# A written instruction order from w_out's last norm to gate_up's first pair, with GpSimd making two of the four sums of h2

## The chip, the cores and the metric

The kernel runs on one core of one Trainium2 chip. The core has a matrix engine (TensorE, PE in the profile; PEld is its load of the stationary operand), three engines for elementwise work (VectorE = DVE, ScalarE = ACT, GpSimd = POOL), a queue engine that here only issues DMAs (SyncE = SP), and DMA engines that move data between DRAM and SBUF. Each engine works off its own list of instructions in order; instructions of different engines wait for each other through semaphores. The metric is the device time of one execution in microseconds (us); lower is better.

## The reference, cut to what matters

One residual block: a mixer and a feed-forward network, each between two RMS norms.

```python
def rmsnorm(x, g):
    return x * lax.rsqrt(jnp.mean(x * x, axis=-1, keepdims=True) + RMS_EPS) * g

m = mixer(rmsnorm(x, norm_mix_pre), ...)          # ends with merged @ w_out
x = x + rmsnorm(m, norm_mix_post)
h = rmsnorm(x, norm_ffn_pre)
g, u = jnp.split(h @ w_gate_up, 2, axis=-1)        # [1024, 1024] @ [1024, 2 * 2816]
x = x + rmsnorm((jax.nn.silu(g) * u) @ w_down, norm_ffn_post)
```

All in float32, sequence 1024, model width 1024, hidden width 2816. The change lies between the product with w_out and the first columns of gate_up.

## The kernel before, in words

**Products.** TensorE multiplies in a reduced float32, so each operand is split into a high part (a copy by ScalarE, `copy`) and a low part (source minus high, by VectorE, `sub`); `split` (118) does both, and `mm3` (123) adds high x high, high x low and low x high into one PSUM bank. An operand's low is needed from the third matmul of a product on. `prod` (445) is four such triples: 12 matmuls 128x512, one *product* in what follows.

**gate_up as pairs.** The columns of w_gate_up are taken in 22 pairs f: 128 gate columns and the 128 up columns that belong to them. One pair is a 2x2 block product with the two halves of the sequence, done with seven products in place of eight (Strassen's scheme in Winograd's form). Its weight operands are A11 and A12 (gate columns, lower and upper half of the contraction), A22 and four sums S1 to S4; its operands of h are B11, B21, B22 and four sums T1 to T4. `prep_first` (397) loads the gate columns (`raw`, 512 KB) and splits them; `prep_rest` (408) loads the up columns, makes S1 to S4 (into `sx`, `raw` and `s4`) and splits them. `strassen` (474) does the products in the order S2, S1, S3, S4, A22 and joins them by additions into c12, c22 and c21; with each bank that is read, a bank comes free for a later product. B11 and B21, the first half of the sequence, stand as `hah`/`hal`; B22 as `hch`/`hcl`; T1 to T4 as `hth`/`htl` with blocks 0 to 3.

**The stage of the change.** w_out is done in eight tiles of 128 rows: `e_mm` (1179) makes a tile's two banks `pm`, `e_norm` (1198) follows one tile later: two Squares by ScalarE out of PSUM, the factor (`rms_scale` 177, a Sqrt by ScalarE among five small ones by VectorE), two multiplications with the gain (`tt`), the addition to x, a store of x2 by GpSimd's queue, a third Square, a second factor, one multiplication, and on TensorE eight transposes into two banks, which ScalarE copies to `um` (h, transposed). Tile 7 is the last.

After tile 5 all of B11 and B21 are there, so the products A11 and A12 of the first seven pairs (NPRE = 7) can be done before the second half of the sequence is. `f_first(f)` (1232) does that for pair f: load, split, A11's product, a copy of the bank to `c21`, A12's product added into the same bank, a copy to `c12`, both stored to `pre_dram` by GpSimd's queue. Four of them are written ahead of tile 7's norm, three behind it, between the quarters of `h2_sums` (1267): for each quarter (128 columns of each half of the sequence) VectorE makes two sums u (T1, T2, in `sx`, each needs the one before) and two sums w (T3, T4, in `c22`), all four are split into `hth`/`htl`, and B22's quarter into `hch`/`hcl`.

Then comes the loop over the 22 pairs (1311). For f < NPRE GpSimd's queue loads the two kept products back (1313 to 1316, tiles `c21` and `c11`), `Pairs` prepares the rest of two pairs ahead, and `strassen` does the five products left. The results go through a Sigmoid on ScalarE into `sgf` (1326) and two multiplications on VectorE.

**What sets the order.** A scheduler orders each engine's list by its own estimate of readiness, except where instructions are marked by `tc.keep_in_program_order`: then they stay as written. All engine calls go through the helper `InOrder` (65 to 78), which marks while `strict[0]` is set; so every recorded instruction bears its line, L73. `strict` is on up to the end of the attention part and is set off at 1139, ahead of w_out; from there on, and so in the whole stage, the scheduler decides. Buffers bind as well: `raw` has 3, `hi` 4, `lo` 3, `sx` 1, `s4` 1, and `c21`, `c12`, `c22` 2 each; PSUM has six banks here. SyncE's list holds the loads of weights and x, GpSimd's the stores and the loads of `pre_dram`; an issue waits in its list for the buffer that it fills, or for the landing of what it reads back, and holds up what stands behind it.

Of the kernel before, what the change touches and what calls it, by code (L numbers as in the profile page):

```python
# [17 lines left out]
P = 128  # L18
# [27 lines left out]
def block_kernel(  # L46
# [13 lines left out]
    w_down: bass.AP,  # L60
    out: bass.AP,
):
    strict = [False]

    class InOrder:


        def __init__(self, engine):
            self.engine = engine

        def __getattr__(self, name):
            def call(*args, **kw):
                ins = getattr(self.engine, name)(*args, **kw)  # L73
# [7 lines left out]
    nc = SimpleNamespace(  # L81
        **{e: InOrder(getattr(bass_nc, e)) for e in ("tensor", "vector", "scalar", "gpsimd", "sync")}
    )
    x2d = x[0]
    o2d = out[0]
# [20 lines left out]
    def add(o, a, b):  # L106
        nc.vector.tensor_tensor(o, a, b, op=ALU.add)
# [7 lines left out]
    def copy(o, a):  # L115
        nc.scalar.activation(o, a, AF.Copy)
# [280 lines left out]
    def prep_first(src1, there=None):  # L397

        if there is None:
            r1 = raw_t()  # L400
            nc.sync.dma_start(r1, kmaj(src1))
            h1, l1 = hi_t(), lo_t()
            split(h1, l1, r1)
        else:
            r1, h1, l1 = there
        return dict(A11=(h1[:, LO], l1[:, LO]), A12=(h1[:, UP], l1[:, UP])), r1

    def prep_rest(src2, r1):

# [48 lines left out]
    def t_(tmp, name):  # L458
        return tmp.tile([P, NC], F32, tag=name, name=name)
# [335 lines left out]
    for ij, (kind, j, _, _) in enumerate(jobs):  # L795
        if ij == 2:
            logf_pre = forget_sums()
        if ij == 4:
            forget_store(*logf_pre)
        if ij < 2:  # L800
            if ij == 0:
                heads = [
                    prep_first(wcols(a), t) for (_, _, a, _), t in zip(jobs, ((r0, h0, l0), None))
                ]
                firsts = [
                    strassen_first(w, h1b, psm, pp, n == 0) for n, (w, _) in enumerate(heads)
                ]
            (w, r1), (c11, p1) = heads[ij], firsts[ij]
            w = {**w, **prep_rest(wcols(jobs[ij][3]), r1)}
            if ij == 1:  # L810
                pairs.q.append(pairs.prep(*pairs.srcs.popleft()))
            _, c12, c21, c22 = strassen(w, h1b, psm, pp, p1)
        elif ij < len(jobs) - 1:
            if ij == 12:
                k_load(0)
                q_load(0)
                cb_of(0, 0)
                cb_of(0, 1)
            c11, c12, c21, c22 = strassen(pairs.get(), h1b, psm, pp)
        else:  # L820
            w = pairs.get()
            psm_close()
            strict[0] = True
            pss, pss_close = pool("pss", space=PSUM)
            c11, c12, c21, c22 = last_pair(w)
        if kind == "qk":
            so = pp.tile([P, NC], F32, tag="so", name="so")
            copy(so, c11)
            for r, c, t in ((0, n1, so), (0, n2, c12), (1, n1, c21), (1, n2, c22)):
                nc.gpsimd.dma_start(qk_dram[j][r, :, c], t)  # L830
        elif kind == "z":
            zt = z_tile("zt")
            mul(zt[:, n1], c21, c11)
            mul(zt[:, n2], c12, c22)
            zts[j] = zt
        elif kind == "gb":
            for m, parts in ((j, (c11, c12)), (j + 1, (c21, c22))):
                zt = zts.pop(m)
                for n in range(2):
                    o = n * NC  # L840
                    ot = pp.tile([P, NC], F32, tag="so", name="ot")
                    nc.vector.tensor_scalar(
                        ot, zt[:, o : o + NC], cw[:, 2, m : m + 1], None, op0=ALU.mult
                    )
                    for t in (1, 0):
                        lag = 2 - t
                        c = slice(0 if n else lag, NC)
                        nc.vector.scalar_tensor_tensor(
                            ot[:, c], zt[:, o + c.start - lag : o + NC - lag],
                            cw[:, t, m : m + 1], ot[:, c], op0=ALU.mult, op1=ALU.add,  # L850
                        )
                    mul(ot, ot, parts[n])
                    nc.gpsimd.dma_start(ya_dram[m][:, o : o + NC], ot)
        else:
            so = c11
            strict[0] = False
# [27 lines left out]
        return tp_.tile([P, NC], F32, tag="sg", name="sg", bufs=4)  # L884

    t1, t1_close = pool("att1")
    strict[0] = True

    yas = {}

# [245 lines left out]
    divide(3, 1)  # L1136
    yb2.append(halves_of(1))
    yb_split(1, range(4))
    strict[0] = False
    yb_close()  # L1140
    wo_pool, wo_close = pool("wo", side="right")
    woh = wo_pool.tile([P, KT, D], F32R, name="woh")
# [52 lines left out]
        nc.sync.dma_start(xt, x2d[st * P : (st + 1) * P, :])  # L1195
        return xt

    def e_norm(st, pm):
        ss = slice(st * P, (st + 1) * P)
        xt = xts.popleft()  # L1200
        if st + 1 < ST:
            xts.append(load_xt(st + 1))
# [5 lines left out]
        ssq = st_tile("ssq")  # L1208
        add(ssq, s2[:, 0:1], s2[:, 1:2])
        rs = rms_scale(ssq)  # L1210
        for n in range(2):
            ns = slice(n * NC, (n + 1) * NC)
            nc.vector.scalar_tensor_tensor(
                tt[:, ns], pm[n], rs, gpo[:, ns], op0=ALU.mult, op1=ALU.mult
            )
        add(xt, xt, tt)
        nc.gpsimd.dma_start(x2_dram[ss, :], xt)
        ssq = st_tile("ssq")
        nc.scalar.activation(tt, xt, AF.Square, accum_out=ssq)
        rs = rms_scale(ssq)  # L1220
        nc.vector.scalar_tensor_tensor(tt, xt, rs, gpr, op0=ALU.mult, op1=ALU.mult)
        for q in range(2):
# [4 lines left out]
            copy(um[:, 4 * q : 4 * q + 4, ss], tp)  # L1227

    def f_src(f):
        return wgu[:, f * P : (f + 1) * P], wgu[:, FH + f * P : FH + (f + 1) * P]  # L1230

    def f_first(f):
        w, _ = prep_first(f_src(f)[0])
        b1, p1 = strassen_first(w, hb, psm, fp)
        c11 = t_(fp, "c12")
        copy(c11, b1)
        nc.gpsimd.dma_start(pre_dram[f][0], p1)
        nc.gpsimd.dma_start(pre_dram[f][1], c11)

    hb = [(hah[:, q], hal[:, q]) for q in range(2)]  # L1240
    xts = deque([load_xt(0)])
# [1 line left out]
    for st in range(ST):  # L1243
# [12 lines left out]
    wo_close()  # L1256

    hc_pool, hc_close = pool("hc")
    ht_pool, ht_close = pool("ht", side="right")
    hch = hc_pool.tile([P, 4, NC], F32R, name="hch")  # L1260
    hcl = hc_pool.tile([P, 4, NC], F32R, name="hcl")
    hth = ht_pool.tile([P, 4, 4, NC], F32R, name="hth")
    htl = ht_pool.tile([P, 4, 4, NC], F32R, name="htl")
    hb.append((hch, hcl))
    hb += [(hth[:, b], htl[:, b]) for b in range(4)]

    def h2_sums(sl):
        a = slice(sl * P, (sl + 1) * P)
        b = slice(NC + sl * P, NC + (sl + 1) * P)
        b11, b12 = um[:, 0:4, a], um[:, 0:4, b]  # L1270
        b21, b22 = um[:, 4:8, a], um[:, 4:8, b]
        u = wtile("sx", 1).rearrange("p (t k) s -> p t k s", t=2)
        sub(u[:, 0], b12, b11)
        sub(u[:, 1], b22, u[:, 0])
        split(hth[:, 0:2, :, a], htl[:, 0:2, :, a], u)
        for n, x in enumerate(((b22, b12), (b21, u[:, 1]))):
            w = t_(fp, "c22").rearrange("p (k s) -> p k s", k=4)
            sub(w, *x)
            split(hth[:, 2 + n, :, a], htl[:, 2 + n, :, a], w)
        split(hch[:, :, a], hcl[:, :, a], b22)  # L1280

    for sl in range(4):
        if 4 + sl < NPRE:
            f_first(4 + sl)
        h2_sums(sl)


    wd = wdn.rearrange("(k h p) d -> h p k d", h=2, p=P)
# [17 lines left out]
        for o, t in ops.items():  # L1306
            nc.gpsimd.dma_start(a_dram[o][k // 2][k % 2], t)

    rest = Pairs([f_src(f) for f in range(NPRE)], prep_rest_alone)
    whole = Pairs([f_src(f) for f in range(NPRE, NF)])  # L1310
    for f in range(NF):
        if f < NPRE:
# [10 lines left out]
        sgs = z_tile("sgf")  # L1323
        for g, u, ns in ((g1, u1_, n1), (g2, u2, n2)):
            sg = sgs[:, ns]
            nc.scalar.activation(sg, g, AF.Sigmoid)
            mul(sg, sg, g)
            mul(yf[:, ns], sg, u)
        if f % 2:
# [258 lines left out]
```

## Time and profile before

| | |
|---|---|
| median of 3 runs | 1348.56 us (1348.53 to 1348.72) |
| profiled execution, its own time | 1347.07 us |
| its span, first to last instruction | 1345.3 us |
| GpSimd's instructions in the span | 252, of which 64 masks 128x128 and no sum of 128x512 |
| DMA traffic over the span | 138 GB/s |
| columns of w_gate_up: loads of 512 KB | 51, median 3.7 us to landing |

How to read it: the profile is of one execution; times in its rows are us from the start of the span. A row of the timeline is start, duration, engine, line, operation, output <- inputs by the program's names, shape, and in brackets the idle time before it with what ended it. The chain of waits is followed back from the last instruction of the program, at each step to what released it. A row of the groups gives count, busy us, mean ns of one. The waits give an engine's idle time by instruction and releaser: total, count, longest. A windows row is a stretch, its length, then the busy us of TensorE, its weight load, VectorE, ScalarE, GpSimd, and then the mean granted TensorE clock (1 is full speed), the DMA engines' share and GB/s.

### The profile page before, as it was taken

Reading aid. Unit: us, or ns where it says so; the run is one execution under the profiler, and the core shown is the slowest. Engines: PE = TensorE matmul, PEld = TensorE weight load, DVE = VectorE, ACT = ScalarE, POOL = GpSimd, SP = SyncE. Lnnn points to the kernel's source line nnn. Section 1 sums busy time; section 2 is a strip of 40 time slices with the busy share of each in tenths; the row PEclk is TensorE's granted clock in tenths of the full one; section 3 lists DMA queues with packets and bytes.
Section 4 is the critical chain, followed back from the end, with each engine's and each line's share of the span. In section 5 each row is a group of like instructions: output and inputs, shape, how many; then the busy total and the mean of one; then the engine's idle time right before and its main releaser. Section 6 shows DMA issues by size and latency. Waiting matters only on the chain. (4 is left out here: it accounts for less than half of the span.)

```text
span 1345.3 us, 17661 instructions
## 1 busy us (share of the span) xinstructions
PE 1319.8 (98%) x6725; PEld 1094.4 (81%) x6725; DVE 934.2 (69%) x1450; ACT 534.6 (40%) x853; POOL 127.2 (9%) x252
## 2 busy tenths in 40 slices
PE   7999999999999999999999999999999999999997
PEld 6978888888888778788887788888888888888886
DVE  6874668754556766675668898777677766677585
ACT  6642222243345756523537322223222323444452
POOL 0001000011112112000002121110111011000000
PEclk9999999999999999999999999999999999999999
DMA  7242422333326445462235554232333236965541
GB/s 220 92 120 87 126 71 71 102 125 110 102 80 194 157 141 172 121 219 78 95 110 188 176 189 159 103 108 72 117 103 117 96 109 239 355 246 194 161 165 63
DMA packets 153397, 186.86 MB, mean 139 GB/s; under 512 B 9424, under 2 KB 106768, under 8 KB 153312
## 3 DMA queue, kind: packets, MB, share of 16 engines
q1 hardware_dynamic: 138576, 137.19, 32.9%
q0 software_dynamic: 14736, 48.54, 9.5%
q8 instruction: 52, 0.85, 0.3%
q14 instruction: 33, 0.27, 0.1%
HBM read 136.62 MB, written 49.09 MB: 138 GB/s over the span
## 5 line engine op out<-in xcount | busy, mean ns | idle before, releaser
L73 DVE TENSOR_TENSOR c<-c,b 128x512 f32<-128x512 f32 x195 | 133.1, 682 | 85.1 <-PE b L73 66.9
L73 DVE TENSOR_TENSOR lo<-raw,hi 128x1024 fp32r<-128x1024 f32 (+1 forms) x93 | 112.1, 1205 | 77.9 <-PE b L73 68.5
L73 ACT ACTIVATE hi<-raw 128x1024 fp32r<-128x1024 f32 (+1 forms) x100 | 101.7, 1018 | 128.8 <-PE b L73 77.7
L73 PE MATMUL b<-hth,hi 128*128 128x512 f32 x352 | 137.0, 389 | 0.2 <-DVE c L73 0.2
L73 PE MATMUL b<-hth,lo 128*128 128x512 f32 x352 | 137.0, 389 | 0.2 <-DVE lo L73 0.2
L73 PE MATMUL b<-htl,hi 128*128 128x512 f32 x352 | 136.9, 389 | 0.0
L73 ACT ACTIVATE hi<-sx 128x1024 fp32r<-128x1024 f32 x41 | 43.5, 1062 | 228.8 <-PE b L73 203.7
L73 PEld LDWEIGHTS b<-hth,hi 128*128 128x128 f32 x352 | 66.1, 188 | 14.3 <-DVE c L73 0.6
L73 PEld LDWEIGHTS b<-hth,lo 128*128 128x128 f32 x352 | 66.1, 188 | 14.2 <-DVE lo L73 0.6
L73 PEld LDWEIGHTS b<-htl,hi 128*128 128x128 f32 x352 | 66.1, 188 | 13.7
L73 DVE TENSOR_TENSOR lo<-sx,hi 128x1024 fp32r<-128x1024 f32 x41 | 50.2, 1224 | 32.0 <-PE b L73 30.5
L73 PE MATMUL b<-hah,hi 128*128 128x512 f32 x176 | 68.7, 393 | 1.9 <-ACT c L73 1.9
L73 DVE TENSOR_TENSOR sx<-raw 128x512 f32<-128x512 f32 x78 | 53.7, 688 | 22.8 <-DMA raw<-in_w_in_dram 11.9
L73 PE MATMUL b<-hal,hi 128*128 128x512 f32 x176 | 68.5, 389 | 0.0
L73 PE MATMUL b<-hah,lo 128*128 128x512 f32 x176 | 68.4, 389 | 0.0
L73 PE MATMUL pd<-hi,lo 128*128 128x512 f32 x160 | 62.3, 389 | 0.0
L73 PE MATMUL pd<-hi 128*128 128x512 f32 x160 | 61.9, 390 | 0.0
L73 PE MATMUL pd<-ghi 128*128 128x512 f32 x148 | 57.7, 390 | 0.0
L73 PE MATMUL pd<-ghi,glo 128*128 128x512 f32 x148 | 57.6, 389 | 0.0
L73 PE MATMUL pd<-glo,ghi 128*128 128x512 f32 x148 | 57.6, 389 | 0.0
L73 PE MATMUL b<-hT12h,hi 128*128 128x512 f32 x136 | 53.0, 390 | 0.6 <-ACT hi L73 0.6
L73 PE MATMUL b<-hT34h,hi 128*128 128x512 f32 x136 | 53.2, 391 | 0.4 <-DVE c L73 0.4
(363 smaller groups left out, 3358.2 us busy)
## 6 DMA issues: line engine op xcount, KB each, us to landing
raw<-in_w_gate_up_dram SPq DMA_DIRECT2D x51, 512.0 KB, 3.7
raw<-in_w_in_dram SPq DMA_DIRECT2D x35, 512.0 KB, 3.9
a_dramS<-um POOLq DMA_DIRECT2D x44, 256.0 KB, 2.6
a_dramA<-um POOLq DMA_DIRECT2D x33, 256.0 KB, 2.7
xt<-in_x_dram SPq DMA_DIRECT2D x16, 512.0 KB, 4.7
sg<-sg_dram SPq DMA_DIRECT2D x32, 256.0 KB, 4.2
graw<-a_dramS SPq DMA_DIRECT2D x14, 512.0 KB, 3.8
sg_dram<-c POOLq DMA_DIRECT2D x24, 256.0 KB, 2.3
```

The lines of the kernel that those rows point to most:

```text
L73: ins = getattr(self.engine, name)(*args, **kw)
```

## The change

The stage from the first halves of pairs 0 and 1 to the last split of pair 1's operands gets a written order.

- `strict` becomes a tuple of engine names, so single engines can be held to the order; from behind the first two loads and splits up to pair 0's last split all five are held, and afterwards only ScalarE for pair 0's two Sigmoids.
- `e_norm` is cut into `e_x2` (with a second part, `then`), `e_sq`, `e_h2` and `e_turn`, `f_first` into the class `First` (load, `high`, `low`, `one`, `two`, `keep`), `h2_sums` into `u_sum`, `w_sum`, `u_high`, `u_low`, `w_split`, `b_split`, and `prep_rest` gets a twin in steps, `rest_steps` (s4 is summed ahead of the splits there, and split ahead of the raw tile).
- The parts are called one by one. Tile 7's norm, which was written behind four first halves, begins ahead of the first; A11 and A12 products of different pairs take turns; the quarters' sums are spread over the first halves; B22's splits all come together near the end; pair 0's rest is prepared in four steps between the last first halves.
- The two w sums of each quarter move from VectorE to GpSimd.

```diff
-    strict = [False]
+    engines = ("tensor", "vector", "scalar", "gpsimd", "sync")
+    strict = [()]
-                if strict[0] and ins is not None:
+                if self.name in strict[0] and ins is not None:
                     tc.keep_in_program_order(ins)
...
+    def rest_steps(src2, r1):
+        r2 = raw_t()
+        nc.sync.dma_start(r2, kmaj(src2))
+        yield
...
+        sub(s3, a11, a21)
+        add(s1, a21, a22)
+        sub(s2, s1, a11)
+        sub(s4, a12, s2)
+        yield
+        split(hx, lx, sx)
+        yield
+        split(h4, l4, s4)
+        yield
+        split(h2, l2, r2)
...
+    class First:
+        def __init__(self, f):
+            self.f, self.raw = f, raw_t()
+            nc.sync.dma_start(self.raw, kmaj(f_src(f)[0]))
+        def high(self):
+            copy(self.h, self.raw)
+        def low(self):
+            sub(self.l, self.raw, f32(self.h))
+        def one(self):
+            prod(self.b, (self.h[:, LO], self.l[:, LO]), hb[B11], True)
+        def two(self):
+            prod(self.b, (self.h[:, UP], self.l[:, UP]), hb[B21], False)
+        def keep(self, n):
+            t = t_(fp, "c12" if n else "c21")
+            copy(t, self.b)
+            nc.gpsimd.dma_start(pre_dram[self.f][n], t)
...
-    for f in range(4):
-        f_first(f)
-    e_norm(ST - 1, prev)
...
+    def w_sum(sl):
+        a, b = ab(sl)
+        ws[sl] = []
+        for n, x in enumerate(((um[:, 4:8, b], um[:, 0:4, b]), (um[:, 4:8, a], us[sl][:, 1]))):
+            w = t_(fp, "c22").rearrange("p (k s) -> p k s", k=4)
+            nc.gpsimd.tensor_tensor(w, *x, op=ALU.subtract)
+            ws[sl].append(w)
...
+    F = [First(f) for f in range(2)]
+    for f in F:
+        f.high()
+        f.low()
+    strict[0] = engines
+    for f in range(2, 4):
+        F.append(First(f))
+    u_sum(0)
+    w_sum(0)
+    x2_last = e_x2(ST - 1, prev)
+    F[0].one()
+    F[1].one()
+    F[0].keep(0)
+    F[2].high()
+    x2_last = x2_last()
+    u_high(0)
+    F[1].keep(0)
+    ssq_last = e_sq(*x2_last)
+    F[2].low()
+    F.append(First(4))
+    u_low(0)
+    F[3].high()
+    e_h2(*x2_last, ssq_last)
+    F[0].two()
+    F[0].keep(1)
+    u_sum(1)
+    F[3].low()
+    F.append(First(5))
+    F[2].one()
+    w_split(0)
+    F[2].keep(0)
+    w_sum(1)
+    u_high(1)
+    F[1].two()
+    F[1].keep(1)
+    e_turn(ST - 1, x2_last[1])
+    u_low(1)
+    u_sum(2)
+    F[4].high()
+    F[4].low()
+    F.append(First(6))
+    F[3].one()
+    F[3].keep(0)
+    w_split(1)
+    w_sum(2)
+    u_high(2)
+    u_low(2)
+    u_sum(3)
+    F[2].two()
+    F[2].keep(1)
+    F[5].high()
+    F[5].low()
...
+    F[4].one()
+    F[4].keep(0)
+    u_high(3)
+    w_split(2)
+    w_sum(3)
+    u_low(3)
+    F[3].two()
+    F[3].keep(1)
+    F[6].high()
+    F[6].low()
+    g0 = rest_steps(f_src(0)[1], g0_r1)
+    next(g0)
...
+    b_split(0)
+    b_split(1)
+    F[5].one()
+    F[5].keep(0)
+    b_split(2)
+    b_split(3)
+    F[4].two()
+    F[4].keep(1)
+    next(g0)
+    w_split(3)
+    F[6].one()
+    F[6].keep(0)
+    next(g0)
+    F[5].two()
+    F[5].keep(1)
+    next(g0)
+    F[6].two()
+    F[6].keep(1)
+    g0 = next(g0)
+    strict[0] = ()
...
-    for sl in range(4):
-        if 4 + sl < NPRE:
-            f_first(4 + sl)
-        h2_sums(sl)
...
-    rest = Pairs([f_src(f) for f in range(NPRE)], prep_rest_alone)
+    rest = Pairs([f_src(f) for f in range(1, NPRE)], prep_rest_alone)
+    rest.q.append(g0)
...
+            if f == 0:
+                strict[0] = ("scalar",)
             nc.scalar.activation(sg, g, AF.Sigmoid)
+            strict[0] = ()
```

More of the change, by code (lines that the diff above doesn't have):

```diff
@@ L62, in block_kernel, with __init__ @@
 ):
-    strict = [False]
+    engines = ("tensor", "vector", "scalar", "gpsimd", "sync")
+    strict = [()]
     class InOrder:
-        def __init__(self, engine):
-            self.engine = engine
+        def __init__(self, name):
+            self.name, self.engine = name, getattr(bass_nc, name)
         def __getattr__(self, name):
@@ L81, in block_kernel @@
     nc = SimpleNamespace(
-        **{e: InOrder(getattr(bass_nc, e)) for e in ("tensor", "vector", "scalar", "gpsimd", "sync")}
+        **{e: InOrder(e) for e in engines}
     )
@@ L406, in prep_first @@
         return dict(A11=(h1[:, LO], l1[:, LO]), A12=(h1[:, UP], l1[:, UP])), r1
+    def rest_steps(src2, r1):
+        r2 = raw_t()
+        nc.sync.dma_start(r2, kmaj(src2))
+        yield
+        a11, a12, a21, a22 = r1[:, LO], r1[:, UP], r2[:, LO], r2[:, UP]
+        sx = wtile("sx", 1)
+        s2, s3 = sx[:, LO], sx[:, UP]
+        sub(s3, a11, a21)
+        s1 = a21
+        add(s1, a21, a22)
+        sub(s2, s1, a11)
+        s4 = s4_t()
+        sub(s4, a12, s2)
+        yield
+        hx, lx = hi_t(), lo_t()
+        split(hx, lx, sx)
+        yield
+        h4, l4 = s4h_t(), s4l_t()
+        split(h4, l4, s4)
+        yield
+        h2, l2 = hi_t(), lo_t()
+        split(h2, l2, r2)
+        yield dict(
+            S2=(hx[:, LO], lx[:, LO]), S3=(hx[:, UP], lx[:, UP]),
+            S1=(h2[:, LO], l2[:, LO]), A22=(h2[:, UP], l2[:, UP]),
+            S4=(h4, l4),
+        )
     def prep_rest(src2, r1):
@@ L855, in block_kernel @@
             so = c11
-            strict[0] = False
+            strict[0] = ()
             if ij < len(jobs) - 1:
@@ L886, in block_kernel @@
     t1, t1_close = pool("att1")
-    strict[0] = True
+    strict[0] = engines
     yas = {}
@@ L1138, in block_kernel @@
     yb_split(1, range(4))
-    strict[0] = False
+    strict[0] = ()
     yb_close()
@@ L1196, in load_xt, with e_x2 @@
         return xt
-    def e_norm(st, pm):
-        ss = slice(st * P, (st + 1) * P)
+    def e_x2(st, pm):
         xt = xts.popleft()
@@ L1210, in e_norm, with then, e_sq, e_h2 @@
         rs = rms_scale(ssq)
[L1211 to L1217, printed above, removed]
+        def then():
+            for n in range(2):
+                ns = slice(n * NC, (n + 1) * NC)
+                nc.vector.scalar_tensor_tensor(
+                    tt[:, ns], pm[n], rs, gpo[:, ns], op0=ALU.mult, op1=ALU.mult
+                )
+            add(xt, xt, tt)
+            nc.gpsimd.dma_start(x2_dram[st * P : (st + 1) * P, :], xt)
+            return xt, tt
+        return then
+    def e_sq(xt, tt):
         ssq = st_tile("ssq")
         nc.scalar.activation(tt, xt, AF.Square, accum_out=ssq)
+        return ssq
+    def e_h2(xt, tt, ssq):
         rs = rms_scale(ssq)
         nc.vector.scalar_tensor_tensor(tt, xt, rs, gpr, op0=ALU.mult, op1=ALU.mult)
+    def e_turn(st, tt):
         for q in range(2):
@@ L1226, in e_norm @@
                 nc.tensor.transpose(tp[:, k, :], tt[:, kt * P : (kt + 1) * P], ident)
-            copy(um[:, 4 * q : 4 * q + 4, ss], tp)
+            copy(um[:, 4 * q : 4 * q + 4, st * P : (st + 1) * P], tp)
+    def e_norm(st, pm):
+        xt, tt = e_x2(st, pm)()
+        e_h2(xt, tt, e_sq(xt, tt))
+        e_turn(st, tt)
     def f_src(f):
         return wgu[:, f * P : (f + 1) * P], wgu[:, FH + f * P : FH + (f + 1) * P]
[L1232 to L1238, printed above, removed]
+    class First:
[3 more added lines that the diff above has]
+        def high(self):
+            self.h = hi_t()
+            copy(self.h, self.raw)
+        def low(self):
+            self.l = lo_t()
+            sub(self.l, self.raw, f32(self.h))
+        def one(self):
+            self.b = bank(psm, "b1")
+            prod(self.b, (self.h[:, LO], self.l[:, LO]), hb[B11], True)
[5 more added lines that the diff above has]
+            nc.gpsimd.dma_start(pre_dram[self.f][n], t)
     hb = [(hah[:, q], hal[:, q]) for q in range(2)]
@@ L1251, in block_kernel, with ab, u_sum @@
         prev = cur
-    for f in range(4):
-        f_first(f)
-    e_norm(ST - 1, prev)
-    ep_close()
-    wo_close()
+    wo_close()
+    ht_pool, ht_close = pool("ht", side="right")
+    hth = ht_pool.tile([P, 4, 4, NC], F32R, name="hth")
+    htl = ht_pool.tile([P, 4, 4, NC], F32R, name="htl")
+    us, ws = {}, {}
+    def ab(sl):
+        return slice(sl * P, (sl + 1) * P), slice(NC + sl * P, NC + (sl + 1) * P)
+    def u_sum(sl):
+        a, b = ab(sl)
+        u = us[sl] = wtile("sx", 1).rearrange("p (t k) s -> p t k s", t=2)
+        sub(u[:, 0], um[:, 0:4, b], um[:, 0:4, a])
+        sub(u[:, 1], um[:, 4:8, b], u[:, 0])
@@ new lines, in w_sum, with u_high, u_low, w_split @@
+    def w_sum(sl):
+        a, b = ab(sl)
+        ws[sl] = []
[3 more added lines that the diff above has]
+            ws[sl].append(w)
+    def u_high(sl):
+        copy(hth[:, 0:2, :, ab(sl)[0]], us[sl])
+    def u_low(sl):
+        a = ab(sl)[0]
+        sub(htl[:, 0:2, :, a], us[sl], f32(hth[:, 0:2, :, a]))
+    def w_split(sl):
+        a = ab(sl)[0]
+        for n, w in enumerate(ws[sl]):
+            split(hth[:, 2 + n, :, a], htl[:, 2 + n, :, a], w)
@@ new lines, in b_split @@
+    def b_split(sl):
+        a, b = ab(sl)
+        split(hch[:, :, a], hcl[:, :, a], um[:, 4:8, b])
+    F = [First(f) for f in range(2)]
+    for f in F:
+        f.high()
+        f.low()
+    strict[0] = engines
+    for f in range(2, 4):
[12 more added lines that the diff above has]
+    F[2].low()
@@ L1258, in block_kernel @@
+    u_sum(3)
[3 more added lines that the diff above has]
+    F[5].low()
+    g0_r1 = raw_t()
+    nc.sync.dma_start(g0_r1, kmaj(f_src(0)[0]))
+    F[4].one()
[10 more added lines that the diff above has]
+    next(g0)
     hc_pool, hc_close = pool("hc")
-    ht_pool, ht_close = pool("ht", side="right")
     hch = hc_pool.tile([P, 4, NC], F32R, name="hch")
@@ L1261, in block_kernel @@
     hcl = hc_pool.tile([P, 4, NC], F32R, name="hcl")
-    hth = ht_pool.tile([P, 4, 4, NC], F32R, name="hth")
-    htl = ht_pool.tile([P, 4, 4, NC], F32R, name="htl")
+    b_split(0)
[17 more added lines that the diff above has]
+    g0 = next(g0)
+    strict[0] = ()
     hb.append((hch, hcl))
@@ L1265, in block_kernel @@
     hb += [(hth[:, b], htl[:, b]) for b in range(4)]
[L1267 to L1280, printed above, removed]
@@ L1325, in block_kernel @@
             sg = sgs[:, ns]
+            if f == 0:
+                strict[0] = ("scalar",)
             nc.scalar.activation(sg, g, AF.Sigmoid)
+            strict[0] = ()
             mul(sg, sg, g)
```

1 line of the change is left out of this document (removed).

## The prediction, as put on record before the changed kernel ran

> **What bounds the kernel now.** I read the page first, then all waits of TensorE (PE), then five-microsecond windows, and the timelines and the chain around the change.
>
> ```profile
> span 1345.3 us, 17661 instructions
> PE 1319.8 (98%) x6725; PEld 1094.4 (81%) x6725; DVE 934.2 (69%) x1450; ACT 534.6 (40%) x853; POOL 127.2 (9%) x252
> ...
> PE tp L73 <- DVE hn L73: 7.9, 1, 7.9
> PE b L73 <- ACT c L73: 1.9, 1, 1.9
> ...
> 725.00:730.00 5.00, 3.09 (x16) 2.33 (x15) 2.25 (x5) 3.64 (x6) 0.88 (x3) 1.00 0.83 293
> ...
> 758.51 370.21 PE b L73 x1632
> ```
>
> PE is busy for 98% of the span. Its longest wait, 7.9 us, is the kernel's start; the next, 1.9 us, lies in the stage of the change (725 to 730 us; the granted clock there is 1.00). The last row is the chain's: from 758.51 us on PE runs 1632 products in one piece. So 758.51 us, the first matmul of pair 0's A22 product, is my mark: what moves it moves the end, and nothing before it counts otherwise.
>
> ```profile
> 704.86 0.48 PE L73 MATMUL b<-hah,hi 128*128 128x512 f32 x1
> ...
> 726.52 0.39 PE L73 MATMUL b<-hah,lo 128*128 128x512 f32 x1
> 728.81 0.50 PE L73 MATMUL b<-hah,hi 128*128 128x512 f32 x1 [1.91 <-ACT c L73]
> ...
> 730.30 0.39 PE L73 MATMUL b<-hah,hi 128*128 128x512 f32 x1
> 733.02 0.39 PE L73 MATMUL b<-hah,hi 128*128 128x512 f32 x1
> ...
> 752.70 0.39 PE L73 MATMUL b<-hth,hi 128*128 128x512 f32 x1
> 757.91 0.39 PE L73 MATMUL b<-hch,s4l 128*128 128x512 f32 x1
> 758.51 0.50 PE L73 MATMUL b<-hth,hi 128*128 128x512 f32 x1 [0.21 <-DVE c L73]
> ```
>
> 730.30 and 733.02 lie twelve matmuls apart, so a product costs 2.72 us and a matmul 0.227. Between 704.86 and 752.70 stand sixteen products (two for each of seven first halves, S2, S1) and eight transposes (0.79, from 704.07 to 704.86 for the set before). Without a wait that is 704.86 + 16 x 2.72 + 0.79 + two starts of 0.09 = 749.35; the trace has 752.70. S3 and S4 follow (5.44): PE alone could be at the mark at 754.8, against 758.51. **The most that can be won is 3.7 us.** It goes to the 1.91, to smaller waits, and to late starts behind them.
>
> ```profile
> 726.35 1.28 ACT L73 ACT_TABLE_LOAD   x1 [2.15 <-DMA x_dram<-xt]
> 727.64 0.63 ACT L73 ACTIVATE sgf<-c 128x512 f32<-128x512 f32 x1
> 728.18 0.58 ACT L73 ACTIVATE c<-b 128x512 f32<-128x512 f32 x1
> ```
>
> The 1.91 us is ScalarE's: pair 0's Sigmoid stands far too early, waits 2.15 us for a DMA, loads a table, and only then comes the copy that frees PE's bank.
>
> **The change, part by part.** The built instructions show that it does what it says: SyncE's order is the same, PE's products no longer mix, and behind pair 0 all queues agree but for names.
>
> *Removed.* The Sigmoid of pair 0 now follows the last split of pair 1 on ScalarE: the wait, the 1.28 and the 0.63 leave the path, and with them up to 2.1 us. What becomes late next is worked out below.
>
> *The norm of tile 7.*
>
> ```profile
> 694.14 0.60 ACT L73 ACTIVATE tt<-pm 128x512 f32<-128x512 f32 x1
> 702.23 1.28 DVE L73 SCALAR_TENSOR_TENSOR tt<-xt,r,gpr 128x1024 f32<-128x1024 f32 x1
> ...
> 704.07 1.03 PE L73 MATMUL tp<-ident,tt 128*128 128x128 f32 x8
> ...
> 705.00 1.07 ACT L73 ACTIVATE um<-tp 128x512 f32<-128x512 f32 x2
> ...
> 705.96 0.60 ACT L73 ACTIVATE tt<-pm 128x512 f32<-128x512 f32 x1
> 722.62 1.28 DVE L73 SCALAR_TENSOR_TENSOR tt<-xt,r,gpr 128x1024 f32<-128x1024 f32 x1
> ```
>
> Tile 6 took 9.4 us from its first Square to its end, tile 7 17.9, since lows and sums stood between. In the new order only two lows of 1.22 stand between, one us later than the norm needs them, and F2's high, which held up the two copies of um (705.00), no longer stands ahead of the Square: it starts some 0.3 sooner, 705.65 + 9.4 + 0.8 = 715.9. Five products have started PE at 704.86, so it wants to transpose at 718.5: no wait, 2.6 us of cover. Likewise F2's low is there at 712.2 (wanted 713.6), F3's at 718.3 (wanted 719.9); the copies that free banks have over 1.5 us each.
>
> *GpSimd's sums.* A quarter's four sums shared VectorE; now GpSimd (POOL) makes the w pair. VectorE sheds 8 x 0.60 us, but one buffer holds u and two hold w, so VectorE's u sums of quarter s+1 wait for POOL's second w of s, and POOL waits for VectorE's lows of the w before. On POOL the w pair is queued behind DMA issues.
>
> ```profile
> L73 DVE TENSOR_TENSOR htl<-c,hth 128x512 fp32r<-128x512 f32 x8 | 5.5, 681 | 0.0
> L73 DVE TENSOR_TENSOR lo<-raw,hi 128x1024 fp32r<-128x1024 f32 x8 | 9.8, 1220 | 1.6 <-PE pm L73 0.8 <-PE b L73 0.6 <-ACT hi L73 0.2
> 734.14 0.68 DVE L73 TENSOR_TENSOR htl<-c,hth 128x512 fp32r<-128x512 f32 x1
> 734.74 0.69 DVE L73 TENSOR_TENSOR hcl<-um,hch 128x512 fp32r<-128x512 f32 x1
> ...
> 747.35 0.70 DVE sx L73
> 748.08 0.70 DVE raw L73
> ...
> L73 POOL TENSOR_TENSOR cb<-cb,mask 128x128 f32<-128x128 f32 x64 | 28.9, 459 | 103.3 <-DVE nm L73 99.1 <-DMA cb<-c_dram 4.0
> masks.py:65 POOL MEMSET tri<- 128x128 f32 x1 | 0.2, 205 | 0.0
> L73 POOL MEMSET s<- 128x8 f32 x1 | 0.1, 122 | 0.0
> ...
> pre_dram<-c POOLq DMA_DIRECT2D x14, 256.0 KB, 4.2
> DMA to landing us min/median/max: 2.2/3.5/6.8
> ...
> 743.20 4.03 DMA raw<-in_w_gate_up_dram
> ...
> 750.25 4.21 DMA raw<-in_w_gate_up_dram
> DMA to landing us min/median/max: 3.7/3.9/5.7
> ```
>
> On VectorE a 512 op takes a step of 0.60 (734.14 to 734.74), 0.72 where it needs the one before (747.35 to 748.08), a 1024 op 1.14 to 1.22. POOL has no 512 sum in this trace. The mask row is a 128 sum, 459 ns; the two memsets leave about 116 ns without elements, so 512 would be 0.116 + 4 x 0.343 = 1.49. Bounds: 0.69, as on VectorE, and 4 x 0.459 = 1.84. I take **1.5**. A first half's store is 4.2 us from issue to landing (2.2 to 6.8).
>
> [...]
>
> Now quarter by quarter. F0.two ends at 713.3, its copy at 714.3, its store lands at 718.5; POOL's next instruction, the reload of F0, waits for that landing, and with one more issue behind it (0.54 each) the w pair of quarter 1 runs from 719.7 to 722.7. VectorE has been idle since 720.65. u of quarter 2: 724.15; F4's low: 725.3. PE starts F4.one at 724.86 and wants the low at its third matmul, 725.3: **0.1** with the restart. Next round: w lows 725.9, POOL's two sums 729.0, u 730.4, F5's low 731.55; PE wants it at 730.9: **0.8**, restart included. This round costs 0.6 + 2 x 1.5 + 1.4 + 1.2 = 6.2 us where PE's two products take 5.44.
>
> *Behind it VectorE stays the late one.* From 731.55: three lows and F6's low (4.1), four lows of hch (2.4), pair 0's four sums (2.85) to 740.8. That frees the slot for pair 1's second raw (SyncE, 4.15 to land): 745.0. In the built order pair 1's sums stand ahead of the low of pair 0's S1 operand; with the s4 low between they take 3.4, and the low 1.1: 749.5. PE starts S1 at 747.55 and wants it at 748.0: **1.6**. S1 ends at 751.9. That low frees the next raw: 753.65; three sums (2.15), a low (1.14) and the c22 addition (0.7) give 757.6; PE has done S3 and S4 at 757.4. The mark comes at **757.6**, 0.9 us before 758.51. Three of the 3.7 us go to new waits.
>
> Two such loads stand in that chain, one in series with the sums of pair 1 and one with those of pair 2; the trace of before has them in the same places (743.20 and 750.25).
>
> *Ends.* With 0.69 for a POOL sum the quarters are hidden, F5's low stands at 728.65, and the mark comes at 755.45: -3.1. With 1.84 it is +0.5; with 1.84 and stores of 6.8 us +3.1. Raw loads of 3.7 or 5.7 shift the chain by -0.9 or +3.1.
>
> **The sum.** The profiled execution took 1347.07 us (1345.3 span, 1.8 around it); the three runs shown have a median of 1348.56, 1.5 above it. I set the change on the median: 1348.56 - 0.9 = **1347.7**.
>
> **Rivals.**
> 1. *The two engines take turns* (slower). Nearly all of VectorE's work here reads two tiles of SBUF, as does a POOL sum. If they can't run side by side, quarter 0's w pair (700.65 on) meets the end of tile 6's norm (702.23): its transposes, 704.07, come 1.35 late. Quarter 1's pair starts behind the u low at 720.65, not 719.7: 1.0. Quarter 2's has the u low between its halves: 1.85. Quarter 3's two sums lie in VectorE's full stream: 3.0. Together +7.2, so 1348.56 - 0.9 + 7.2 = 1354.9. It decides as soon as most of this overlap is lost; half of it gives 1351.3. For it: VectorE is the late engine all through. Neither for nor against: in this trace POOL's 64 masks meet operations of VectorE with a PSUM input, never a two-tile one for longer than a rim.
> [...]
> 2. *All hidden.* POOL sums near 1.0 or less and early landings: -2.0 to -3.1, time 1346.0 (1345.5 to 1346.5). Against it: the mask's 459 ns at a quarter of the size.
> 3. *Stores land late, sums are slow:* 1.84 and about 6 us: +2.2, time 1350.8. The stores of this stage share the queues with x2's 512 KB, and 6.8 was seen.
>
> **How the numbers follow.** Forecast 0.40, turns 0.38, hidden 0.14, late 0.08. 0.2% is 2.7 us, about what a measurement of this kernel can tell from no change. Slower: turns, of which nearly all lies beyond 2.7, and a third of late: 0.40. Faster: most of hidden and a rim of the forecast: 0.13. Same: 0.47. The range reaches from the hidden case to the priced end of turns, 1345.2 to 1355.0; the forecast's own is 1345.8 to 1349.5.
>
> **What would show it.** Right: no table load before the last of pair 1's splits; no PE wait of 1.9 on ScalarE; PE waits for VectorE's lows at F4.one, F5.one and S1; POOL sums of about 1.5 us; the mark near 757.6. Turns: POOL sums far longer than 1.5 or stretched VectorE rows beside them, and tile 6's transposes later than 704.07. Hidden: only the S1 wait left. Wrong altogether: a wait of PE behind the mark, or another order of the quarters' bound than VectorE and POOL.

## The result, and the profile after

The changed kernel takes **1353.31 us** (median of 6 runs, 1352.86 to 1355.01) against 1348.55 (6 runs) before: a ratio of 1.0042, 95% interval 1.0032 to 1.0053, so it is 4.8 us (0.4%) slower. The forecast was 1347.7, 0.9 below the kernel before. The profiled execution took 1353.0, with a span of 1351.2.

The first two lines are of the page of the changed kernel; the others are PE's waits between 700 and 775 us (total, times, longest):

```profile
span 1351.2 us, 17654 instructions
PE 1321.2 (98%) x6725; PEld 1096.2 (81%) x6725; DVE 934.8 (69%) x1442; ACT 534.9 (40%) x853; POOL 140.5 (10%) x260
...
PE b L74 <- DVE lo L74: 6.3, 4, 4.1
PE tp L74 <- DVE tt L74: 0.5, 1, 0.5
```

POOL has eight instructions and 13.3 us more, VectorE eight less, yet VectorE's busy time has not fallen (934.2 before): eight sums of 0.69 us left it, so what stayed got longer. The 1.91 us on ScalarE is gone. In its place PE waits 6.3 us for lows of VectorE. (F4.one is A11's product of pair 4 among the first halves; S1 is pair 0's product with that operand.) Rows of PE's timeline, with the mark as the last, and a window carry most of it:

```profile
704.44 1.09 PE L74 MATMUL tp<-ident,tt 128*128 128x128 f32 x8 [0.51 <-DVE tt L74]
...
733.41 0.50 PE L74 MATMUL b<-hah,lo 128*128 128x512 f32 x1 [1.43 <-DVE lo L74]
...
755.00 0.67 PE L74 MATMUL b<-hth,lo 128*128 128x512 f32 x1 [4.09 <-DVE lo L74]
755.47 0.63 PE L74 MATMUL b<-hth,hi 128*128 128x512 f32 x1
...
764.46 0.40 PE L74 MATMUL b<-hth,hi 128*128 128x512 f32 x1
...
755.00:758.50 3.50, 3.50 (x9) 2.74 (x10) 2.28 (x3) 2.55 (x4) 0.00 (x0) 0.52 0.95 273
```

From the spacing of PE's matmuls, what is above 0.227 is lost: tile 6's transposes 0.67, F4.one 0.55, F5.one 1.70, F6.one 0.82 (for these three with the slow matmul behind the wait), S1 4.25. The last row is a window: behind S1's wait the granted clock is 0.52, so eight matmuls come 0.43 apart in place of 0.23; that adds 1.7. Together these are 9.7 us, where the kernel before loses 3.7 in the stage. The mark, the start of pair 0's A22, is at 764.46, 5.95 behind the kernel before, and the spans differ by 5.9: nothing behind the mark counts.

A u low of the kernel before, what VectorE and GpSimd of the changed kernel did around F5.one (timelines), and its chain of waits that ends at S1:

```profile
733.01 1.22 DVE L73 TENSOR_TENSOR htl<-sx,hth 128x1024 fp32r<-128x1024 f32 x1
...
727.30 2.32 DVE L74 TENSOR_TENSOR htl<-sx,hth 128x1024 fp32r<-128x1024 f32 x1
730.80 0.69 DVE L74 TENSOR_TENSOR sx<-um 128x512 f32<-128x512 f32 x1 [1.18 <-POOL c L74]
...
726.87 1.67 POOL L74 TENSOR_TENSOR c<-um 128x512 f32<-128x512 f32 x1 [2.22 <-DVE htl L74]
728.50 2.27 POOL L74 TENSOR_TENSOR c<-um,sx 128x512 f32<-128x512 f32 x1
...
744.85 5.49 DMA raw<-in_w_gate_up_dram
753.73 1.23 DVE lo L74
755.00 379.56 PE b L74 x1666
```

The u low takes 2.32 us, 1.22 before; the GpSimd sum beside it takes 2.27. That is rival 1's picture, and read as turns the rows fit: the first sum ends at 728.5, the u low 1.22 behind it would end at 729.7 (729.62 in the row), and a sum of 1.29, its length with nothing in its way, behind that at 730.9 (730.77). The chain shows a second thing: a load of 5.49 us and, behind it, a low that PE needs.

### The profile page after: what moved, and what is told of

The parts are those of the page before. It is cut to its first block, busy times and chain, and to the rows that moved or that the text cites. A ratio compares the mean times of both kernels' runs of the same rounds, so it can differ in the third digit from the quotient of the medians.

```text
span 1351.2 us, 17654 instructions
## 1 busy us (share of the span) xinstructions
PE 1321.2 (98%) x6725; PEld 1096.2 (81%) x6725; DVE 934.8 (69%) x1442; ACT 534.9 (40%) x853; POOL 140.5 (10%) x260
## 4 chain that ended last, share of the span: by engine, by line
PE 58%; DVE 3%; ACT 1%; issue 1%; POOL 0%; DMA 0%; DVEq 0%; ACTq 0%; POOLq 0%
PE b L74 28%; PE pd L74 16%; PE pm L74 5%; PE pbb L74 3%; PE pba L74 2%; PE po L74 1%; PE tps L74 1%; PE sp L74 1%; DVE lo L74 1%; DVE htl L74 0%; DVE tt L74 0%; ACT tt L74 0%; POOL c L74 0%; DMA raw<-in_w_gate_up_dram 0%; PE tp L74 0%
## 5 line engine op out<-in xcount | busy, mean ns | idle before, releaser
L74 DVE TENSOR_TENSOR sx<-raw 128x512 f32<-128x512 f32 x78 | 53.7, 688 | 23.1 <-DMA raw<-in_w_in_dram 11.9
```

## The experiments

Theory L: GpSimd's sums and VectorE's operations on two SBUF tiles take turns. Theory O: the order costs the time, above all pair 1's sums ahead of the low of pair 0's S1 operand. Each group of kernels ran beside the kernel before on one chip; its median there was 1346.3 to 1348.5, so kernels of different groups are compared by their ratios. The first first half starts between 704.2 and 707.0 us in these profiles, so waits are compared, not the times at which rows stand.

| kernel | w sums | S1's low | median us | ratio to before (95%) |
|---|---|---|---|---|
| changed | GpSimd | behind pair 1's sums | 1353.31 | 1.0042 (1.0032 to 1.0053) |
| e1_w_on_vector | VectorE | behind | 1346.14 | 0.9987 (0.9979 to 0.9996) |
| e2_low_first | GpSimd | ahead | 1348.03 | 1.0000 (0.9991 to 1.0009) |
| e3_both | VectorE | ahead | 1344.32 | 0.9973 (0.9963 to 0.9983) |

**e1_w_on_vector**

```diff
-            nc.gpsimd.tensor_tensor(w, *x, op=ALU.subtract)
+            sub(w, *x)
```

> The changed kernel with all eight w sums back on VectorE, at the same places of the written order. Theory L (GpSimd's sums and VectorE's operations on two SBUF tiles take turns, and VectorE also waits for GpSimd to be done with w before it may overwrite u): VectorE's stretched rows of 2.3 us go back to 1.22 and its idle times before u (2.4 and 1.2 us) vanish, which is more than the 4.8 us of sums that it takes back; PE's waits at F4.one, F5.one and F6.one (0.55, 1.70 and 0.82 us with restarts) vanish or shrink below 0.3 each, the wait at S1 stays or shrinks a little because pair 1's sums still stand ahead of S1's low: 1349.5 us (1348.3 to 1350.5). Theory O (the written order alone costs the time, GpSimd is a help): VectorE has 4.8 us more to do, the waits stay or grow: 1353 us or more.

1346.14, lower than either theory said. VectorE's rows (timeline) are back, and the load is shorter (chain):

```profile
726.25 1.22 DVE L74 TENSOR_TENSOR htl<-sx,hth 128x1024 fp32r<-128x1024 f32 x1
...
728.84 1.22 DVE L74 TENSOR_TENSOR lo<-raw,hi 128x1024 fp32r<-128x1024 f32 x1
...
740.56 3.66 DMA raw<-in_w_gate_up_dram
```

All waits at F4 to F6 are gone with 4.8 us more work on VectorE, so O alone is out. S1's low starts at 747.14, PE loses about 1.5 us there and 1.1 at the mark, where it waits for an addition, and no matmul runs at half clock. I had expected S1's wait to stay; with VectorE in time and a load shorter by 1.8 us it shrank from 4.25.

**e2_low_first, e3_both.** The order by which all five engines are held ends at pair 0's last split; pair 1's sums and splits are the scheduler's, and it put the sums among pair 0's lows. A flag puts pair 1's first sum under VectorE's written order, which already holds the low.

```diff
+        was = strict[0]
+        if held[0]:
+            strict[0], held[0] = ("vector",), False
         sub(s3, a11, a21)
+        strict[0] = was
...
+            held[0] = f == 0
             _, g2, u1_, u2 = strassen(rest.get(), hb, psm, fp, p1)
```

> The changed kernel, with pair 1's first sum held behind the low of pair 0's S1 operand on VectorE (both kept in program order); GpSimd still makes the w sums. Theory O: the wait of 4.3 us at S1 is owed to pair 1's sums standing ahead (they wait for a load until 750.3, while the low's high is there at 749.4), and the eight matmuls behind it at a granted clock of about half cost 1.6 more; both go, the waits of 3.1 us at F4 to F6 stay: 1347.5 us (1346.8 to 1348.5). Theory L alone (VectorE is simply late by the turns, whatever stands first): the wait at S1 shrinks by less than half: 1350.5 us or more.

> Both edits: all sums of h2 on VectorE and S1's low ahead of pair 1's sums. If both L and O hold, the savings add up: no wait of PE over 0.5 us between 705 us and the mark, the mark at about 755.3 us: 1345.5 us (1344.8 to 1346.8), faster than before and after. If only L holds: as the first kernel; if only O holds: as the second or slower.

PE's waits in the stage, e2 first, then e3:

```profile
PE b L74 <- DVE lo L74: 2.3, 3, 1.4
```

```profile
PE b L74 <- DVE c L74: 0.6, 1, 0.6
```

In e2 the waits at F4 to F6 stand as in the changed kernel (2.3), the one at S1 and the half clock are gone: 5.3 us, and the time is where theory O has it. In e3 no wait is left before the mark (the 0.6 us is at pair 1's A22): from its first first half to the mark PE takes 50.1 us, 59.2 in the changed kernel, 53.7 before. Its time is 0.5 us below the range. The savings don't add up: putting the sums back is worth 7.2 us with the late low and 3.7 with the early one, since both edits take from S1's wait and both end the half clock.

**e4_before_gpsimd**: in the kernel before, the one line `sub(w, *x)` becomes `nc.gpsimd.tensor_tensor(w, *x, op=ALU.subtract)`.

> The kernel before with one part of the change alone: the w sums on GpSimd, the scheduler's order otherwise (it moves VectorE's list by itself, and the early Sigmoid stays). Theory L: stretched rows of VectorE and POOL sums of 1.3 to 2.3 us; slower than before by 1 to 4 us: 1351 us. Theory O: the relief of VectorE counts: 1346.5 to 1348.5 us.

1350.91, ratio 1.0024 (1.0015 to 1.0034): this part alone costs 2.4 us, in the scheduler's order too. VectorE's and GpSimd's timelines and the waits of ScalarE and PE:

```profile
719.88 2.30 DVE L73 TENSOR_TENSOR lo<-raw,hi 128x1024 fp32r<-128x1024 f32 x1
...
718.84 2.26 POOL L73 TENSOR_TENSOR c<-um 128x512 f32<-128x512 f32 x1
...
ACT hth L73 <- POOL c L73: 4.3, 3, 2.2
...
PE b L73 <- ACT c L73: 3.4, 4, 1.8
```

The same turns; here the price goes through ScalarE, which waits for w and has PE's bank copies behind it (3.4 us of PE, 1.9 before). The scheduler also moved VectorE's list, and PE loses 1.4 us ahead of S3, for an addition, so the 2.4 us are the turns' and the new list's together.

**e5_sigmoid_alone**: in the kernel before, pair 1's last split and pair 0's Sigmoids are put under ScalarE's written order, as the change does for the Sigmoids.

> The kernel before with one part of the change alone: on ScalarE, pair 0's two Sigmoids are held behind pair 1's last split; nothing else is written. If the prediction's first step is right, PE's wait of 1.91 us on ScalarE and the restart behind it go and nothing else becomes late: 1346.6 us (1346.2 to 1347.2). If VectorE is late anyway in the scheduler's order, the wait comes back before the mark: 1348.5 us.

1345.81 against 1347.23, ratio 0.9989 (0.9980 to 0.9998), close to the 0.9986 that the forecast amounts to: the wait on ScalarE is gone, and 1.4 of the 1.9 us arrive. PE's only listed wait left in the stage is 0.6 us for an addition at the mark.

**e8_free_sigmoid**: e3_both with the Sigmoids left to the scheduler.

> The kernel with both edits, but pair 0's Sigmoids left to the scheduler, which puts the first with its table load back among the first halves' copies on ScalarE. If the Sigmoid's place is a part of the gain: 1346.2 us (1.9 more than 1344.3) and a wait of PE on ScalarE of about 2 us. If the written order has made it harmless: 1344.3 us.

Ratio 0.9989 (0.9981 to 0.9998), where e3_both has 0.9973 and, repeated, 0.9974: some 2 us. It shows as a wait of PE for a low of VectorE, not on ScalarE as I had expected: the Sigmoid waits 1.96 us for a reload, its table load (1.28) follows, the splits' highs stand behind both, and VectorE's lows come late behind the highs.

```profile
PE b L74 <- DVE lo L74: 1.5, 1, 1.5
```

**e6_two_u**

```diff
-        u = us[sl] = wtile("sx", 1).rearrange("p (t k) s -> p t k s", t=2)
+        u = us[sl] = (flat2(z_tile("u")) if sl % 2 else wtile("sx", 1)).rearrange("p (t k) s -> p t k s", t=2)
```

> The changed kernel, GpSimd making the w sums, but with a second buffer for u in the odd quarters, so that VectorE's next u need not wait until GpSimd has read this one; the buffer is taken from those of the reloads, which puts the first reload behind GpSimd's sums. Theory L (turns): the stretched rows of 2.3 us stay, the idle times of VectorE before u (2.4 and 1.2 us) go: half of the loss against the kernel with VectorE's sums stays: 1349.5 us (1348 to 1351). Theory D (the wait of VectorE for GpSimd's reading is the whole price): as with the sums on VectorE, 1346.1 us. If the wait for u was covered anyway: 1353 us.

Ratio 1.0050 (1.0036 to 1.0064): not faster, so theory D is out, and my half as well. VectorE no longer waits ahead of u, but its u sum now meets GpSimd's second w and takes 1.78 in place of 0.69. VectorE's and GpSimd's timelines, PE's waits, and a window behind S1's wait:

```profile
721.64 2.33 DVE L74 TENSOR_TENSOR htl<-u,hth 128x1024 fp32r<-128x1024 f32 x1
723.89 1.78 DVE L74 TENSOR_TENSOR sx<-um 128x512 f32<-128x512 f32 x1
...
722.85 2.26 POOL L74 TENSOR_TENSOR c<-um,u 128x512 f32<-128x512 f32 x1
...
PE b L74 <- DVE lo L74: 5.9, 3, 4.1
...
755.00:761.50 6.50, 5.37 (x13) 4.21 (x14) 4.11 (x6) 3.68 (x5) 0.00 (x0) 0.50 0.55 163
```

At F4 to F6 PE loses 2.6 us where it lost 3.1: most of the wait for the buffer had been the wait for the turn under another name, and about 0.5 was the buffer's own. The time doesn't show the 0.5. In this profile the half clock behind S1's wait (4.25, as in the changed kernel) lasts 6.8 us and costs 2.6, where it cost 1.7. The first reload also stands elsewhere here, at 732.62 in place of 719.52; this run doesn't separate that.

**e7_probe**: e3_both with five instructions per pair that feed nothing.

```diff
+        for _ in range(5):
+            if f % 3 == 1:
+                nc.gpsimd.tensor_tensor(pb, pa, pa, op=ALU.subtract)
+            elif f % 3 == 2:
+                nc.gpsimd.tensor_copy(pb, pa)
+            else:
+                nc.gpsimd.memset(pb, 1.0)
```

> The kernel with both edits (sums on VectorE, S1's low first), and in the loop over the pairs, where TensorE has no gap, five extra GpSimd instructions on 128x256 per pair that feed nothing: by turns a difference of a tile with itself, a copy, a memset. If GpSimd and VectorE take turns, GpSimd's sum and copy and VectorE's operations on two SBUF tiles show stretched rows where they meet and none where VectorE has an operand in PSUM, and the memset meets VectorE without stretch. If they run side by side, every form keeps one duration. The time itself is not what this run is for: some us about 1344.3.

The probe's tile (duration in ns: least, median, most), a group of VectorE with one operand in PSUM behind 760 us, and two rows of VectorE beside GpSimd's sums, then beside its memsets:

```profile
L74 POOL MEMSET pb<- x48: 311/312/315, 568.4 to 1107.6; 128x256 f32 x48
L74 POOL TENSOR_TENSOR pb<-c x35: 607/942/1141, 768.6 to 1088.4; 128x256 f32<-128x256 f32 x35
L74 POOL COPY pb<-c x35: 396/401/933, 782.7 to 1105.3; 128x256 f32<-128x256 f32 x35
...
L74 DVE TENSOR_TENSOR c<-c,b 128x512 f32<-128x512 f32 x100 | 68.0, 680 | 24.9 <-PE b L74 24.4
...
857.14 0.99 DVE L74 TENSOR_TENSOR raw<-raw 128x512 f32<-128x512 f32 x1
858.05 0.67 DVE L74 TENSOR_TENSOR c<-c,b 128x512 f32<-128x512 f32 x1
...
936.21 0.68 DVE L74 TENSOR_TENSOR sgf<-sgf,c 128x512 f32<-128x512 f32 x1
936.81 1.22 DVE L74 TENSOR_TENSOR lo<-raw,hi 128x1024 fp32r<-128x1024 f32 x1
```

GpSimd's sum goes from 607 to as much as 1141 ns and its copy, which reads one tile, from 396 to 933; the memset, which reads none, never moves (48 rows, 311 to 315). All 11 copies that met no VectorE operation on two SBUF tiles took 396 to 402. Of the 24 that met one, the nine that had started first took 396 to 402 too, and the 15 that had started second 708 to 933: the one that starts first keeps its time. On VectorE, of the 128x512 operations between 760 and 1112 us, 57 on two tiles that met a reading GpSimd instruction took 677 to 1102 ns, 137 that met none 675 to 694, ten that met only a memset 678 to 693, and 16 with a PSUM operand that met a reading one 672 to 689.

**e9_memset_w**: the changed kernel with `nc.gpsimd.memset(w, 0.5)` in the place of the w sums; T3 and T4 are left out.

> The changed kernel, every instruction at its place, but GpSimd's eight w sums replaced by memsets of the same tiles (T3 and T4 are left out, a constant stands for them): GpSimd still writes w at its place in its queue, but reads nothing from SBUF. If it is the turns at reading that cost (theory L), VectorE's rows of 2.3 us go back to 1.22 and, with 4.8 us less to do on VectorE, S1's low is in time although pair 1's sums stand ahead of it: 1344.5 us (1343.8 to 1346). If the cost lies in GpSimd's queue (issues and reloads ahead of w) or in the written order, the waits of PE stay: 1351 us or more.

1346.54 against 1347.31, ratio 0.9997 (0.9988 to 1.0005). VectorE's rows are at 1.22 and PE has no wait at F4 to F6, as L says. But the time is 2.0 us above my figure, by the ratio 3.6, and that lies at S1. PE's waits, the load that pair 1's sums wait for (chain), and two windows behind S1's wait:

```profile
PE b L74 <- DVE lo L74: 1.9, 1, 1.9
...
739.30 5.75 DMA raw<-in_w_gate_up_dram
...
749.00:751.00 2.00, 1.29 (x6) 1.07 (x7) 2.00 (x3) 1.98 (x3) 0.00 (x0) 1.00 0.63 183
751.00:754.50 3.50, 3.50 (x10) 2.77 (x9) 2.28 (x4) 1.29 (x2) 0.00 (x0) 0.53 0.85 252
```

The load is the one that took 5.49 in the changed kernel, with no turns about. PE loses 2.15 us at S1, and 1.5 us later 3.4 us at half clock cost 1.6 more. So part of S1's wait is the order's and the load's, and relief of VectorE without turns was worth nothing here beyond e1.

**e10_c22_first, e11_both_again**: e3_both with pair 1's addition to c22 held ahead of pair 3's sums (the same marks on VectorE), and e3_both again beside it.

> The kernel with both edits (sums on VectorE, S1's low first), and pair 1's addition of S3's product to c22 held ahead of pair 3's sums on VectorE: that addition is what PE waits for 0.6 us, with a restart, at pair 1's A22. If it stands alone there: 1343.5 us, 0.7 below the kernel with both edits; if the scheduler's order behind it becomes late elsewhere: 1344.3 us or more.

> The kernel with both edits once more, beside the other two on the same chip: 0.9973 of the kernel before (0.9963 to 0.9983).

Ratios 0.9980 (0.9971 to 0.9989) and 0.9974 (0.9964 to 0.9984). In e10 PE has no listed wait left from 700 to 790 us, and it isn't faster: the 0.7 us can't be told apart, or goes elsewhere. e3_both is the fastest version found, 3 to 4 us below the kernel before.

**e12_reloads_late**: pair 0's two reloads are put under GpSimd's written order, behind the last store.

```diff
+            if f == 0:
+                strict[0] = ("gpsimd",)
             nc.gpsimd.dma_start(p1, pre_dram[f][0])
...
+            strict[0] = ()
```

> The changed kernel, with the reloads of pair 0's two kept products held behind the last store of the first halves on GpSimd's queue; the w sums stay on GpSimd and pair 1's sums ahead of S1's low. Theory Q (the queue and the DMAs share in the price): the reload that stood ahead of quarter 1's w sums and waited for a landing no longer holds them (they start at about 719.5 instead of 720.62, the wait of 0.55 us at F4.one goes), and the load that pair 1's sums wait for, 5.49 us in the changed kernel and 3.66 where no reload was issued just ahead of it, takes about 4.0: the wait at S1 is 1.5 us shorter or more: 1350.8 us (1350 to 1351.8). If only the turns and the order count: 1353.3 us (1352.5 to 1354).

1351.05, but the kernel before is at 1346.27 on this chip: ratio 1.0033 (1.0021 to 1.0045), where the changed kernel has 1.0042. By the time alone nothing is decided. The trace (PE's waits, GpSimd's second w and the load by the chain) says more:

```profile
PE b L74 <- DVE lo L74: 4.3, 3, 2.4
...
720.73 2.28 POOL c L74
...
744.26 3.72 DMA raw<-in_w_gate_up_dram
```

The load is 3.72, and S1's wait 1.7 us shorter; half clock follows it all the same. At F4.one PE still loses 0.38 us, 0.55 in the changed kernel. GpSimd's first w of quarter 1 stands sooner, but then meets VectorE's lows and takes 1.61: the pair ends at 723.00 where it ended at 723.59, and this kernel's stage began 0.45 us earlier. Ahead of the w sums the reload had cost next to nothing; what it covered was the wait for the turn. Whether its place made the later load short is open.

## Why the prediction was wrong, step by step

- **The Sigmoid: right in mechanism.** In the changed kernel the table load stands behind pair 1's splits; alone the step is worth 1.4 us (e5).
- **The norm of tile 7: right.** PE has no wait at its transposes.
- **GpSimd's sums: the failed step.** It priced a sum at 1.5 us running beside VectorE. With nothing in its way it is quicker, 1.30 and 1.29; beside VectorE it takes 1.67 to 2.28 and makes VectorE's rows of 1.22 into 2.32. The price of two sums was here not their duration on GpSimd but the time that they took out of VectorE's. The waits at F4 and F5, 0.1 and 0.8 in the sum, came to 0.55 and 1.70, and F6.one's 0.82 had not been seen. With the sums back on VectorE (e1), or with memsets in their place that read nothing (e9), all of these are gone.
- **S1: the mechanism right, its size wrong three times over.** Pair 1's sums did stand ahead of the low. But VectorE came 4.0 us late to the point where the slot is freed (744.8 for 740.8), the load took 5.49 for 4.15, and behind the wait of 4.25 (1.6 forecast) the granted clock was 0.52, which cost another 1.7. The load lay inside the 3.7 to 5.7 allowed for; the clock was in no case.
- **The rivals.** Rival 1 came true at 1354.9 forecast, 1353.3 measured. It had a chance of 0.38 beside 0.40 for the forecast, though no row spoke against it and VectorE was the late engine all through; the choice of the likeliest was the error. Its mechanism is in the rows (the u low of 1.22 at 2.32 beside a sum; e7's copies, 396 to 402 ns by themselves and 708 to 933 where they started second), its sum is not, term by term: 1.35 at tile 6 measured 0.67, its later terms came out as waits and as S1, and it lacked the clock; that the total came so near is luck in part. *All hidden* and *late stores* fell: the first with the lows that PE waited for, the second with its two conditions, since a sum alone took 1.30 and not 1.84, and the reload behind F0's second store went out 4.4 us after that store's issue (715.12 and 719.52), which leaves no room for 6.

```profile
700.12 1.30 POOL L74 TENSOR_TENSOR c<-um 128x512 f32<-128x512 f32 x1
...
701.06 1.62 DVE L74 SCALAR_TENSOR_TENSOR t<-r,va 128x1 f32<-128x1 f32 x1
...
708.28 0.22 DVE L74 SCALAR_TENSOR_TENSOR t<-r,va 128x1 f32<-128x1 f32 x1
```

The first two of these rows of the changed kernel are rival 1's first term: a VectorE operation on single columns, 0.22 us in the third row, ends at 702.68, when GpSimd's second sum (701.37 to 702.66) is done.

What stays open: why this load takes 5.45 to 5.75 us in three kernels (changed, e6, e9) and 3.66 to 4.03 in others. In the changed kernel and e6 a reload by GpSimd's queue was issued 2.2 and 2.5 us ahead of it, in e9 one 0.03 behind it, and without the reload it was short (e12). But in the kernel before a load at 750.25 has a reload issued 0.19 behind it and takes 4.21, so the reload alone doesn't settle it. So S1's excess of 2.65 us over the forecast is traced to VectorE's lateness and to this load, and no further.

## What to carry to other kernels

Work given to another engine was no relief here: beside the sums on GpSimd a u low of VectorE took 2.32 us in place of 1.22, and with the sums back on VectorE (e1) the ratio went from 1.0042 to 0.9987. Before moving an SBUF-to-SBUF sum from VectorE to GpSimd, look at what VectorE does in that stretch, and count the sum's time on both engines where it works on two SBUF tiles. When an order is written by hand, the first instructions behind it are still the scheduler's: one sum that waits for a load, put ahead of a low, made the longest wait of the stage (4.25 us). A theory of waits can be checked by removing the buffer: if the waits stay, the buffer was not the cause. The time alone is not enough for that, since a change of clock behind a wait can hide half a microsecond (in e6 half clock cost 2.6 us in place of 1.7, and the 0.5 won at F4 to F6 is not in the time).

## What the runs showed of the hardware

- In e7 GpSimd's copy, with one SBUF input, stretched beside VectorE's operations on two SBUF tiles (396 to 933 ns) as its sum did (607 to 1141); its memset did not (311 to 315).
- In the changed kernel a VectorE operation of 0.22 us took 1.62 and ended 0.02 behind a GpSimd sum of 1.29. Of the copies of e7 that met a VectorE operation on two SBUF tiles, those that started first kept their time (396 to 402 ns), those that started second took 708 to 933.
- TensorE's granted clock fell to about half (0.50 to 0.56 in the windows) at idle times of 4.25 us (the changed kernel, as PE started again; e6, already within the wait), behind 2.52 (e12, one us after the start) and behind 2.04 (e9, 1.5 us after), and not behind 2.06 in the kernel before or 1.97 in e4: of these three waits near two us one cost some 1.6 us more and two did not. Half clock lasted 3.4 us in three kernels (755.2 to 758.6 in the changed one, 751.2 to 754.6 in e9, 753.6 to 757.1 in e12; 1.6 to 1.7 us lost) and twice that in e6 (754.7 to 761.6; 2.6 lost).
